# Output projection as seven half-size products, with sums formed by accumulating transfers in device memory

## The chip, the cores and the metric

The kernel runs on one core of a Trainium2 chip. The core has TensorE (PE, matmuls), VectorE (DVE), ScalarE (ACT), GpSimd (POOL) and SyncE (SP), each with an instruction stream of its own that runs in order; SP issues transfers only, POOL and ACT may issue them too. The metric is the device time of one execution in microseconds (us); lower is better.

## The reference, cut to what matters

One layer over 1024 latent tokens and 256 context tokens, model width 1024. A modulated norm and one input projection feed two groups of four heads: retention, and differential attention (the difference of two softmaxes). Their outputs `y`, 1024 tokens x 1024 columns (retention heads first), go through the output projection, are gated and added to `x`; then come a second norm and an MLP.

```python
y_ret_lat = jax.nn.silu(rg_l) * ret_lat.astype(dtype)
...
y_diff_lat = diff_subln(diff_attention(dq_l, k_all, v_all, lam), subln_g, lambda_init)
out_lat = jnp.concatenate([y_ret_lat, y_diff_lat], axis=-1) @ w_out
...
x = x + g1 * y_lat
h2 = rms_norm(x, norm2_g[l]) * (1.0 + sc2) + sh2
x = x + g2 * conv_ffn(h2, w_up[l], conv_w[l], conv_b[l], w_down[l])
```

## The kernel before, in words

All products are float32 made of three passes: an operand is split into a high part (`hi`, cast on ACT) and a remainder (`lo`, subtraction on DVE or POOL), and `passes` (L133 to L135) multiplies hi by hi, lo by hi and hi by lo, one matmul of 128x512 each.

The order in time is: norms and input projection in blocks (0 to 320 us); block 0 with the retention outputs beside it (320 to 400), then another block; differential attention (445 to 643), 32 units, a unit being 128 query tokens of one head; the output projection (L1263 and after, up to 729); up projection, convolution, down projection, final norm. `beside(generator, rate)` puts steps of another job between the matmuls of a running one, `order_only` fixes an order between two instructions without a wait, and a table `TAU` sets at which point of a unit's 5.75 us period each of its operations stands. Each engine then runs its list in order.

*Retention outputs.* For each pair of chunks of one head POOL multiplies the queries (`qq`), raises a variance to the power −1/2 (`ss`) and normalises (`y`); TensorE turns the result, and it is stored in device memory, split into hi and lo, as `yr_d` (one tensor per half of the tokens). During attention four transfers from POOL's queue (`yT<-yrd`, 1 MB each) load it into `yT`.

*Attention.* For each unit DVE forms a mean square (`ssa`, L965), POOL raises it to the power −1/2 (`ssa`, L966), ACT normalises the unit's output with it (`oa`, L969), TensorE turns the result (`pty`, L974), and ACT and DVE write it into `yT[a][half]` (`a`: hi or lo; eight blocks of 128 columns, heads 4 to 7 from attention; 512 tokens). POOL also issues the loads of queries, keys and values (`qhl`, `ks`, `va`), squares a softmax sum per unit (`e`, L962), and loads the first weights of the output projection (`woraw`) and forms their remainders (`wolo`, L1085).

*Output projection.* For each half `n` of the output columns, eight token tiles `t`, eight slices `k` of the width: 2 x 8 tiles of 24 matmuls into one PSUM bank `po`, two banks in turn. The first ones stand between the last units of attention. DVE multiplies a finished tile by the gate (`gated`, L1277) and adds it to the residual `x1[t]` (L1278), which SP loads from `x`; with the second half comes the second norm of those tokens (`norm2`: square on ACT, power on POOL, two scalings on DVE) and a store. `turned0` transposes the first 512 tokens for the up projection beside tiles 4 to 7 of the second half. The MLP adds weights and activations for its own seven-product form with transfers that accumulate: `dma_start(..., accum_op=ALU.add)` on POOL's queue (L1216, `cmb<-w_up`).

## Time and profile before

| what | value |
|---|---|
| median of 3 runs | 1372.66 us (1372.25 to 1372.69) |
| the profiled execution | 1371.83 us, of which its span 1370.1 |
| granted TensorE clock | 0.998 |
| POOL, 470 to 520 us (attention) | 17.17 of 50 us busy |
| ACT, 470 to 520 us | 44.46 of 50 us busy |
| DMA share, 470 to 520 us | 0.82 |
| matmuls | 7026 |

Busy times are those of the core's engines inside the span. A row of a timeline gives start, length, engine, line of the code, operation, destination `<-` sources (numbers of buffers left out), and in brackets how long the engine stood idle before it and what released it. A row of transfers gives size and the median time from issue to landing.

### The profile page before, as it was taken

How to read it: one execution, taken by the hardware profiler on the slowest of the kernel's cores; microseconds unless marked ns; L12 is line 12 of the kernel's file. 1: busy time of each engine (PE TensorE's matmuls, PEld its weight loads, DVE VectorE, ACT ScalarE, POOL GpSimd, SP SyncE). 2: the span in 40 equal slices, each digit the busy share in tenths (PEclk: the TensorE clock that was granted, in tenths of full speed). 3: DMA queues.
4: the chain of work that ended last, by engine and by line, in shares of the span. 5: the costliest groups of instructions: out<-in, count | busy, mean ns of one | idle time of the engine just before them, and what ended most of it. 6: DMA issues, size and time to landing. Idle time of an engine off the chain costs nothing.

```text
span 1370.1 us, 19739 instructions
## 1 busy us (share of the span) xinstructions
PE 1357.6 (99%) x7026; PEld 1144.4 (84%) x7026; DVE 970.5 (71%) x1475; ACT 731.2 (53%) x1397; POOL 304.4 (22%) x395
## 2 busy tenths in 40 slices
PE   9999999999999999999999999999999999999997
PEld 7788888888988899998888888888888888888886
DVE  4755875425776998896457986677766777799857
ACT  4652312424665889986136555455554555454534
POOL 1210004503665424411201222212222210000001
PEclk9999999999999999999999999999999999999999
DMA  9546887654556868623413898888888875963523
GB/s 375 207 170 212 292 305 246 200 175 141 170 169 192 171 174 184 136 47 135 158 50 89 194 227 223 223 224 215 208 223 215 209 189 169 373 220 116 177 92 123
DMA packets 123546, 260.81 MB, mean 190 GB/s; under 512 B 12660, under 2 KB 34164, under 8 KB 122936
## 3 DMA queue, kind: packets, MB, share of 16 engines
q1 hardware_dynamic: 97880, 201.72, 43.5%
q0 software_dynamic: 24992, 56.40, 21.1%
q10 hardware_dynamic: 576, 1.44, 0.3%
q8 instruction: 55, 0.90, 0.3%
q14 instruction: 43, 0.35, 0.1%
HBM read 197.63 MB, written 56.64 MB: 186 GB/s over the span
## 4 chain that ended last, share of the span: by engine, by line
PE 94%; DVE 2%; ACT 2%; DMA 1%; issue 1%; POOL 0%; POOLq 0%; ACTq 0%; DVEq 0%
PE chain L133 6%; PE chain L135 6%; PE chain L134 6%; PE pv L951 5%; PE c L134 5%; PE c L135 5%; PE c L133 5%; PE pA L919 5%; PE pl L135 4%; PE pl L133 4%; PE pl L134 4%; PE pn L135 3%; PE pn L134 3%; PE pn L133 3%; PE third L135 3%; PE third L133 3%
## 5 line engine op out<-in xcount | busy, mean ns | idle before, releaser
L1216 POOL DMA_DIRECT2D cmb<-w_up x80 | 73.6, 1128 | 176.4 <-DMA cmb<-w_up 142.4
L133 PE MATMUL pl<-hT,whi 128*128 128x512 f32 x256 | 105.5, 412 | 0.0
L133 PE MATMUL chain<-T,whi 128*128 128x512 f32 x264 | 103.0, 391 | 0.0
L134 PE MATMUL chain<-T,whi 128*128 128x512 f32 x264 | 102.9, 390 | 0.0
L135 PE MATMUL chain<-T,wlo 128*128 128x512 f32 x264 | 102.4, 389 | 0.0
L922 DVE TENSOR_REDUCE mt<-pA 128x1 f32<-128x1280 f32 x64 | 95.2, 1489 | 7.5 <-PE pA L919 7.1
L135 PE MATMUL pl<-hT,wlo 128*128 128x512 f32 x256 | 100.2, 391 | 0.0
L134 PE MATMUL pl<-hT,whi 128*128 128x512 f32 x256 | 100.0, 391 | 0.0
L135 PE MATMUL c<-whi,ghl 128*128 128x512 f32 x232 | 90.3, 389 | 0.0
L134 PE MATMUL c<-wlo,ghl 128*128 128x512 f32 x232 | 90.3, 389 | 0.0
L133 PE MATMUL c<-whi,ghl 128*128 128x512 f32 x232 | 90.3, 389 | 0.0
L919 PE MATMUL pA<-ks,qhl 128*128 128x512 f32 (+1 forms) x384 | 89.5, 368 | 0.6 <-ACT p L926 0.5
L926 ACT ACTIVATE p<-pA,mt 128x1280 f32<-128x1280 f32 x64 | 85.4, 1335 | 8.5 <-DVE mt L922 8.5
L1139 ACT CAST whi<-cmb 128x512 fp32r<-128x512 f32 x60 | 37.3, 624 | 82.5 <-PE chain L134 66.8
L919 PEld LDWEIGHTS pA<-ks,qhl 128*128 128x128 f32 x384 | 67.9, 189 | 12.7 <-ACT p L926 1.2
L951 PE MATMUL pv<-va,aT 128*128 128x128 f32 x640 | 77.1, 276 | 0.3 <-ACT aT L945 0.2
L951 PEld LDWEIGHTS pv<-va,aT 128*128 128x128 f32 x640 | 74.0, 192 | 1.2 <-ACT aT L945 0.8
L1139 ACT CAST whi<-wra 128x512 fp32r<-128x512 f32 x54 | 33.1, 622 | 72.1 <-PE third L134 42.3
L134 PE MATMUL third<-yT,whi 128*128 128x512 f32 x168 | 65.4, 389 | 0.0
L133 PE MATMUL third<-yT,whi 128*128 128x512 f32 x168 | 65.4, 389 | 0.0
L135 PE MATMUL third<-yT,wlo 128*128 128x512 f32 x168 | 65.4, 389 | 0.0
L133 PE MATMUL pn<-whi,hT 128*128 128x512 f32 x160 | 64.8, 405 | 0.0
(330 smaller groups left out, 3769.1 us busy)
## 6 DMA issues: line engine op xcount, KB each, us to landing
cmb<-w_up POOLq DMA_DIRECT2D x80, 256.0 KB, 6.1
wm<-w_mod SPq DMA_DIRECT2D x32, 512.0 KB, 5.2
cmb<-w_up SPq DMA_DIRECT2D x60, 256.0 KB, 5.3
raw<-w_in SPq DMA_DIRECT2D x27, 512.0 KB, 5.1
wra<-w_up SPq DMA_DIRECT2D x23, 512.0 KB, 5.5
W<-w_down SPq DMA_DIRECT2D x44, 256.0 KB, 5.9
wrb<-w_up SPq DMA_DIRECT2D x40, 256.0 KB, 3.8
ad<-s SPq DMA_DIRECT2D x20, 512.0 KB, 5.2
```

Source lines behind the costliest of these rows:

```text
L133: mm(ps, lh, rh, start=first, stop=False, skip_group_check=more)
L134: mm(ps, lh, rl, start=False, stop=False, skip_group_check=more)
L135: return mm(ps, ll, rh, start=False, stop=last, skip_group_check=more)
L919: mm(self.pa[m][:, c0:c1], self.q[:, m, i, qs], self.k[:, m, c0:c1], start=(i == 0), stop=(i == 1))
L922: nc.vector.tensor_reduce(out=self.mt[:, m : m + 1], in_=self.pa[m][:, :LK], axis=AX.X, op=ALU.min)
L926: nc.scalar.activation(self.p[m], self.pa[m][:, :LK], AF.Exp, scale=-1.0, bias=self.mt[:, m : m + 1], accum_out=self.s[:, m : m + 1])
L951: mm(self.pv, self.aT[:, c, :], self.v[:, c, :], start=(c == 0), stop=(c == NKT - 1))
L1139: cast = nc.scalar.copy(hi, src)
L1216: nc.gpsimd.dma_start(out=o, in_=src, accum_op=ALU.add)
```

## The change

The projection is cut into halves in all three directions: tokens (first and last 512), width (retention and attention heads) and output columns. Seven products of half size, steps A to G of 48 matmuls each, take the place of eight. Each multiplies a sum of blocks of `y` by a sum of blocks of `w_out`:

- *Weight sums.* `ws_d[0..3]` in device memory: four copies of 1 MB issued by SP near 80 us, then eight accumulating transfers of 512 KB on POOL's queue beside the first four tiles of block 0.
- *Token sums.* `sg_d[0..3]`: the retention outputs of the first token half are stored once, unsplit and with turned sign, in `sg_d[0]`; attention outputs of the second token half get their turned sign by the gain `subg[:, 1]`. In attention, `sg_d[2]` is copied from `yr_d` and takes four accumulating transfers of 512 KB, SP copies it to `sg_d[1]` and `sg_d[3]`, and 32 accumulating transfers of 256 KB from `yT` follow on POOL's queue, as heads finish; a head's row of `sg_d[3]` takes four of them, one after another. Two of the four `yT<-yrd` loads go.
- *Steps.* `sum_operand` loads a sum (1 MB) into `raw0` and splits it on ACT and DVE; weights are loaded and split in seven half blocks (28 slices, 16 before). After a step its four banks are gated and added to or subtracted from `x1`: 28 gates, 16 before, four subtractions on POOL. `c1` are four banks (pools `psB`, `psC`), `c2` four (`psA`); steps A, E, F and G go tile by tile, B, C and D run over the slices outside. `turned0` stands beside F and G.

```diff
-    yr_d = [dr.tile([P, 2, H, 512], F32, name=f"yrd{i}") for i in range(2)]
+    yr_d = dr.tile([P, 2, H, 512], F32, name="yrd")
+    sg_d = [dr.tile([P, H, 512], F32, name=f"sgd{i}") for i in range(4)]
+    ws_d = [dr.tile([P, 4, 512], F32, name=f"wsd{i}") for i in range(4)]
+    A11, A12, A21, A22 = [w_out[i][:, c : c + 4, :] for i in range(2) for c in (0, 4)]
...
+                o = self.g % 2 * 2 * P
+                if self.g // 2 == 0:
+                    nc.scalar.mul(r32(yr[:, 0]), pt, -1.0)
+                    nc.sync.dma_start(out=sg_d[0][:, self.h, o : o + 2 * P].rearrange("p (s l) -> p s l", s=2), in_=r32(yr[:, 0]))
+                    return
                 nc.vector.tensor_tensor(out=yr[:, 1], in0=pt, in1=r32(yr[:, 0]), op=ALU.subtract)
-                o = self.g % 2 * 2 * P
-                nc.sync.dma_start(out=yr_d[self.g // 2][:, :, self.h, o : o + 2 * P].rearrange("p a (s l) -> p a s l", s=2), in_=r32(yr))
+                nc.sync.dma_start(out=yr_d[:, :, self.h, o : o + 2 * P].rearrange("p a (s l) -> p a s l", s=2), in_=r32(yr))
...
+        w_copies = [nc.sync.dma_start(out=ws_d[i][:, :, :], in_=a) for i, a in ((0, A21), (1, A11))]
         natural(wget, ctx_lhs, range(NTC), store_to(dv_row))
+        w_copies += [nc.sync.dma_start(out=ws_d[i][:, :, :], in_=a) for i, a in ((2, A11), (3, A12))]
+        for ins, before in zip(w_copies, (-4, -3, -2, -1)):
+            order_only(ins.ins, stops[before].ins)
...
+            for i in range(2):
+                nc.vector.tensor_scalar(out=subg[:, i, :], in0=cl[:, COL_SUB : COL_SUB + H], scalar1=(1 - 2 * i) * (1.0 - LAMBDA_INIT) * SQP, scalar2=None, op0=ALU.mult)
...
-        transposed(wg, None, rtab, 64, 1.0, 0, by_head)
+        w_terms = [(0, A22), (2, A21), (1, ws_d[0]), (3, ws_d[1])]
+
+        def weight_sum(n):
+            if n < 4:
+                i, a = w_terms[n]
+                for k in (0, 2):
+                    added = nc.gpsimd.dma_start(out=ws_d[i][:, k : k + 2, :], in_=a[:, k : k + 2, :], accum_op=ALU.add)
+                    order_only(added.ins, newest[0].ins)
+
+        transposed(wg, None, rtab, 64, 1.0, 0, by_head, each=weight_sum)
...
-    def out_weights(n, sl, eng=nc.sync, low=nc.vector, lag=0):
+    def out_weights(srcs, sl, eng=nc.sync, low=nc.vector, lag=0):
         raws = []
-        for k in range(KD + lag):
-            if k < KD:
+        srcs = [src[:, k, :] for src in srcs for k in range(4)]
...
-    wo_gen = out_weights(0, wo_first, nc.gpsimd, nc.gpsimd, 2)
-
+    wo_gen = out_weights((A11, ws_d[0]), wo_first, nc.gpsimd, nc.gpsimd, 2)
+
+    sums_at = {}
+    for n, src in ((8, yr_d[:, 1]), (10, sg_d[0])):
+        sums_at[n] = [([sg_d[2][:, h : h + 2, :]], src[:, h : h + 2]) for h in (0, 2)]
+    for u in range(3, n_units, 4):
+        h, half = u // NT, u % NT // 4
+        n = {3: 14, 7: 15}.get(u, u + 6)
+        for a in range(2):
+            sums_at.setdefault(n + (2 if u < n_units - 5 else 1) * a, []).append(([sg_d[i][:, h, :] for i in ((1, 0, 3), (3,))[half]], r32(yT[a][half][:, H + h, :])))
+
+    def sum_up(ds, src):
+        for d in ds:
+            nc.gpsimd.dma_start(out=d, in_=src, accum_op=ALU.add)
...
-            if n in (8, 10, 12, 14):
-                a, i = divmod(n // 2 - 4, 2)
+            if n in (8, 10):
                 with tc.issue_after(units[n - 5].pool_ins.ins):
-                    nc.gpsimd.dma_start(out=yT[a][i][:, 0:H, :], in_=yr_d[i][:, a])
+                    nc.gpsimd.dma_start(out=yT[n // 2 - 4][1][:, 0:H, :], in_=yr_d[:, n // 2 - 4])
+            if n == 6:
+                nc.sync.dma_start(out=sg_d[2][:, :, :], in_=yr_d[:, 0])
+            if n == 12:
+                for i in (1, 3):
+                    nc.sync.dma_start(out=sg_d[i][:, :, :], in_=sg_d[2][:, :, :])
+            with tc.issue_after(units[max(0, min(n - 5, n_units - 1))].pool_ins.ins) if n in sums_at else nullcontext():
+                for d, src in sums_at.get(n, ()):
+                    sum_up(d, src)
...
-    psA = ctx_r.enter_context(tc.tile_pool(name="psA", bufs=4, space=PSUM))
+    psA, psC, psB = [ctx_r.enter_context(tc.tile_pool(name=f"ps{nm}", bufs=n, space=PSUM, reuse_waits="tile")) for nm, n in (("A", 4), ("C", 2), ("B", 2))]
+    pst = psA
...
-        for n in range(2):
-            sl = wo_first if n == 0 else []
-            for _ in wo_gen if n == 0 else out_weights(n, sl):
-                pass
-            for t in range(NT):
-                pt = next(out_cycle).tile([P, 512], F32, name="po3", tag="mm")
-                for k in range(KD):
-                    ins = passes(pt, tuple(yT[a][t // 4][:, k, t % 4 * P : (t % 4 + 1) * P] for a in range(2)), sl[k], k == 0, k == KD - 1)
-                    if (n, t) == (0, 0) and k in (0, 7):
-                        order_only(turns[("T1", n_units - 2) if k == 0 else ("Y", n_units - 1)], ins.ins)
-                    tick()
-                dst = x1[t][:, n * 512 : (n + 1) * 512]
-                gated = wo.tile([P, 512], F32, name="gated")
-                nc.vector.tensor_tensor(out=gated, in0=pt, in1=g1[:, n * 512 : (n + 1) * 512], op=ALU.mult)
-                nc.vector.tensor_tensor(out=dst, in0=gated, in1=dst, op=ALU.add)
...
-                if n == 1:
-                    norm2(t)
...
+    rows0, rows1 = x1[:4], x1[4:]
+    left, right = slice(0, 512), slice(512, D)
+    (Y11, Y21), (Y12, Y22) = (B11, B21), (B22, T1)
+    groups = []
+
+    def out_step(cc, a, sl, first, last, by_tile=False):
+        order = [(k, t) for t in range(4) for k in range(4)] if by_tile else [(k, t) for k in range(4) for t in range(4)]
+        for k, t in order:
+            ins = passes(cc[t], tuple(g[:, k, t * P : (t + 1) * P] for g in a), sl[k], first and k == 0, last and k == 3, not first)
+            groups.append(ins)
+            if len(groups) in (1, 8):
+                order_only(turns[("T1", n_units - 2) if len(groups) == 1 else ("Y", n_units - 1)], ins.ins)
+            tick()
+            if by_tile and k == 3:
+                yield t
...
+    def sum_operand(i, tt, half, turn=False):
+        raw = raw0[:, 4 * half : 4 * half + 4, :]
+        nc.sync.dma_start(out=raw, in_=sg_d[i][:, :, :])
+        for k in range(H):
+            if turn:
+                nc.scalar.mul(tt[0][:, k, :], raw[:, k, :], -1.0)
+                nc.vector.scalar_tensor_tensor(out=tt[1][:, k, :], in0=raw[:, k, :], scalar=-1.0, in1=r32(tt[0][:, k, :]), op0=ALU.mult, op1=ALU.subtract)
+            else:
+                split_to(raw[:, k, :], tt, k)
+
+    def gate(dst, src, part, op, eng=nc.vector):
+        gated = wo.tile([P, 512], F32, name="gated", bufs=2)
+        nc.vector.tensor_tensor(out=gated, in0=src, in1=g1[:, part], op=ALU.mult)
+        eng.tensor_tensor(out=dst[:, part], in0=dst[:, part], in1=gated, op=op)
...
+    run(wo_gen)
+    c1 = [(psB if t < 2 else psC).tile([P, 512], F32, name=f"o1_{t}", tag="bank") for t in range(4)]
+    c2 = [psA.tile([P, 512], F32, name=f"o2_{t}", tag="bank") for t in range(4)]
+    run(out_step(c1, Y12, wo_first[:4], True, True, True))
+    sum_operand(2, Y11, 0)
+    w3 = weights(ws_d[3])
+    run(out_step(c2, Y11, wo_first[4:], True, True))
+    for t in range(4):
+        gate(rows1[t], c1[t], left, ALU.add)
+    sum_operand(1, Y12, 1, True)
+    w6 = weights(ws_d[1])
+    for t in range(4):
+        gate(rows0[t], c2[t], right, ALU.subtract)
+    run(out_step(c2, Y21, w3, False, True))
+    w7 = weights(ws_d[2])
+    sum_operand(0, Y11, 0)
+    for t in range(4):
+        gate(rows0[t], c2[t], left, ALU.add)
+    run(out_step(c1, Y12, w6, False, True))
+    w4 = weights(A22)
+    for t in range(4):
+        gate(rows0[t], c1[t], left, ALU.add)
+        done(t, left)
+    sum_operand(3, Y12, 1)
+    pre = [raw_load("wra" if j < 2 else "wrb", w_up[j]) for j in range(NPRE)]
+    early = [[split_op(a[:, c : c + 4, :]) for c in (0, 4)] for a in pre]
+    for t in out_step(c1, Y11, w7, False, True, True):
+        gate(rows0[t], c1[t], right, ALU.subtract)
+        done(t, right)
+        norm2(t)
+    w2 = weights(A12)
+    raws = [up_load(j) for j in range(NSUM)]
+    for a, b in raws:
+        sums_in_place(a, b)
+    beside(turned0(), 0.36, -2.5)
+    for t in out_step(c1, Y12, w4, False, True, True):
+        gate(rows1[t], c1[t], right, ALU.subtract, nc.gpsimd)
+        done(4 + t, right)
+    c1 = [(psB if t < 2 else psC).tile([P, 512], F32, name=f"o3_{t}", tag="bank") for t in range(4)]
+    for t in out_step(c1, Y22, w2, True, True, True):
+        gate(rows1[t], c1[t], left, ALU.subtract)
+        done(4 + t, left)
+        norm2(4 + t)
```

In POOL's list between two powers of attention (units 10 to 12, head 1; 518 to 534 us in the profile). Before:

```order
L1022 DMA va_5275<-dvd_103 128x10x128
L1109 DMA yT11_4470<-yrd1_152 128x2048
L966 TENSOR_TENSOR ssa_5259<-ssa_5259,mhalf_70 128x1
L1078 DMA woraw_5295<-w_out 128x512
L962 TENSOR_TENSOR e_5341<-sa_5061 128x1
L1078 DMA woraw_5369<-w_out 128x512
L962 TENSOR_TENSOR e_5415<-sa_5129 128x1
L966 TENSOR_TENSOR ssa_5338<-ssa_5338,mhalf_70 128x1
L962 TENSOR_TENSOR e_5489<-sa_5200 128x1
L1085 TENSOR_TENSOR wolo_5366<-woraw_5146,wohi_5365 128x512
L1078 DMA woraw_5443<-w_out 128x512
L966 TENSOR_TENSOR ssa_5412<-ssa_5412,mhalf_70 128x1
```

After, from the last of three additions that take the place of the 1 MB load (`yT00`, `yT01`: high part of the first and second token half, `yT10`, `yT11`: remainders):

```order
L1126 DMA sgd3_155<-yT00_4479 128x512
L989 TENSOR_TENSOR ssa_5277<-ssa_5277,mhalf_70 128x1
L1102 DMA woraw_5315<-w_out 128x512
L985 TENSOR_TENSOR e_5361<-sa_5078 128x1
L1102 DMA woraw_5390<-w_out 128x512
L985 TENSOR_TENSOR e_5436<-sa_5146 128x1
L1126 DMA sgd3_155<-yT01_4480 128x512
L989 TENSOR_TENSOR ssa_5358<-ssa_5358,mhalf_70 128x1
L1126 DMA sgd1_153<-yT10_4481 128x512
L1126 DMA sgd0_152<-yT10_4481 128x512
L1126 DMA sgd3_155<-yT10_4481 128x512
L985 TENSOR_TENSOR e_5513<-sa_5218 128x1
```

Additions now stand ahead of and behind the powers; the fourth into this row follows the next power, and after it three more for the next head.

On DVE, the gates of the output projection. Before, at the first three tiles, each tile's product is read and added before the next is gated:

```order
L1278 TENSOR_TENSOR x1_0_6722<-gated_6776,x1_0_6722 128x512
L1277 TENSOR_TENSOR gated_6805<-po3_6780,g1_4474 128x512
L1278 TENSOR_TENSOR x1_1_6723<-gated_6805,x1_1_6723 128x512
L1277 TENSOR_TENSOR gated_6834<-po3_6809,g1_4474 128x512
L1278 TENSOR_TENSOR x1_2_6724<-gated_6834,x1_2_6724 128x512
```

After, between steps B and C, which both write the banks `o2_0` to `o2_3`:

```order
L1340 TENSOR_TENSOR gated_6979<-o2_0_6801,g1_4486 128x512
L1340 TENSOR_TENSOR gated_6982<-o2_1_6802,g1_4486 128x512
L1341 TENSOR_TENSOR x1_0_6774<-x1_0_6774,gated_6979 128x512
L1109 TENSOR_TENSOR wolo_6976<-woraw_6973,wohi_6975 128x512
L1341 TENSOR_TENSOR x1_1_6775<-x1_1_6775,gated_6982 128x512
L1340 TENSOR_TENSOR gated_6985<-o2_2_6803,g1_4486 128x512
L1340 TENSOR_TENSOR gated_6988<-o2_3_6804,g1_4486 128x512
```

A weight remainder and two subtractions stand between the second gate and the third.

At the end of attention, POOL's last powers. Before:

```order
L962 TENSOR_TENSOR e_6645<-sa_6425 128x1
L966 TENSOR_TENSOR ssa_6599<-ssa_6599,mhalf_70 128x1
L962 TENSOR_TENSOR e_6672<-sa_6493 128x1
L966 TENSOR_TENSOR ssa_6642<-ssa_6642,mhalf_70 128x1
L966 TENSOR_TENSOR ssa_6669<-ssa_6669,mhalf_70 128x1
```

After:

```order
L985 TENSOR_TENSOR e_6689<-sa_6465 128x1
L1126 DMA sgd1_153<-yT00_4479 128x512
L1126 DMA sgd0_152<-yT00_4479 128x512
L1126 DMA sgd3_155<-yT00_4479 128x512
L989 TENSOR_TENSOR ssa_6640<-ssa_6640,mhalf_70 128x1
L1126 DMA sgd1_153<-yT10_4481 128x512
L1126 DMA sgd0_152<-yT10_4481 128x512
L1126 DMA sgd3_155<-yT10_4481 128x512
L985 TENSOR_TENSOR e_6719<-sa_6533 128x1
L989 TENSOR_TENSOR ssa_6686<-ssa_6686,mhalf_70 128x1
L989 TENSOR_TENSOR ssa_6716<-ssa_6716,mhalf_70 128x1
```

Six additions of head 3 stand ahead of the last `e`. SP's load of `x1_4`, the first residual of step A, waits for that `e`.

More of the change, by code (lines that the diff above doesn't have):

```diff
@@ L466, in natural_copy, with transposed @@
                 nc.sync.dma_start(out=kvg_d[1 + 2 * hf + i][:, h, 0], in_=st[:, 2 * i : 2 * i + 2, :])
-        def transposed(wget, dst, rtab, blk, scale, col0, order, nat=False, eng=nc.vector):
+        def transposed(wget, dst, rtab, blk, scale, col0, order, nat=False, eng=nc.vector, each=None):
             todo = None
@@ L478, in transposed @@
                 todo = (xa, h, hf) if nat else None
+                if each is not None:
+                    each(2 * h + hf)
             return todo
@@ L908, in __init__ @@
                 self.h, self.qt = divmod(i, NT)
-                self.gain = subg[:, self.h : self.h + 1]
+                self.gain = subg[:, self.qt // 4, self.h : self.h + 1]
                 self.mt = al.tile([P, 2], F32, name="mt", bufs=3)
@@ L1071 @@
     g1 = wo.tile([P, D], F32, name="g1")
-    def out_weights(n, sl, eng=nc.sync, low=nc.vector, lag=0):
+    def out_weights(srcs, sl, eng=nc.sync, low=nc.vector, lag=0):
         raws = []
-        for k in range(KD + lag):
-            if k < KD:
+        srcs = [src[:, k, :] for src in srcs for k in range(4)]
+        for k in range(len(srcs) + lag):
+            if k < len(srcs):
                 raw = wo.tile([P, 512], F32, name="woraw", bufs=4)
-                eng.dma_start(out=raw, in_=w_out[n][:, k, :])
+                eng.dma_start(out=raw, in_=srcs[k])
                 raws.append(raw)
@@ L1082, in out_weights @@
                 whi = wo.tile([P, 512], F32R, name="wohi", bufs=9)
-                wlo = wo.tile([P, 512], F32R, name="wolo", bufs=9)
+                wlo = wo.tile([P, 512], F32R, name="wolo", bufs=8)
                 nc.scalar.copy(whi, raws[k - lag])
@@ L1188, in turned @@
     def turned(hf, d, raw, on_act):
-        pt = pst.tile([P, 512], F32, name="pt3", tag="tr")
+        pt = pst.tile([P, 512], F32, name="pt3", tag="bank")
         for i in range(4):
@@ new lines, in run, with weights @@
+    def run(g):
+        for _ in g:
+            pass
+    def weights(src):
+        sl = []
+        run(out_weights((src,), sl))
+        return sl
+    def sum_operand(i, tt, half, turn=False):
[7 more added lines that the diff above has]
+                split_to(raw[:, k, :], tt, k)
@@ L1291 @@
+    beside(iter(()), 0.0)
     x1lS.close()
@@ L1363 @@
             first[j] = first_sum(chain[j], second[j])
-    pstS.close()
-    psC = ctx_r.enter_context(tc.tile_pool(name="psC", bufs=2, space=PSUM, side="right"))
     ops.append(up_sums(NSUM))
```

22 lines of the change are left out of this document (4 added, 18 removed).

## The prediction

> **What bounds the kernel now.** I read the page first: busy time, then the chain that ended last.
>
> ```profile
> span 1370.1 us, 19739 instructions
> ...
> PE 1357.6 (99%) x7026; PEld 1144.4 (84%) x7026; DVE 970.5 (71%) x1475; ACT 731.2 (53%) x1397; POOL 304.4 (22%) x395
> ...
> PE 94%; DVE 2%; ACT 2%; DMA 1%; issue 1%; POOL 0%; POOLq 0%; ACTq 0%; DVEq 0%
> ```
>
> TensorE is busy for 99% of the span and carries 94% of the chain, so a matmul taken away is time taken away, unless something else then makes TensorE wait. POOL's 22% is an average, and the change loads POOL in two stages only. So next come windows (columns: PE, PEld, DVE, ACT, POOL busy us, granted clock, DMA share, GB/s): one in differential attention, two in the output projection, one in the retention outputs.
>
> ```profile
> 520.00:550.00 30.00, 30.00 (x224) 27.83 (x223) 26.53 (x37) 27.92 (x66) 13.54 (x23) 1.00 0.68 166
> 654.00:680.00 26.00, 26.00 (x117) 21.53 (x116) 11.78 (x16) 3.63 (x6) 8.01 (x6) 1.00 0.39 143
> 680.00:704.00 24.00, 24.00 (x108) 19.88 (x107) 11.22 (x22) 6.80 (x11) 1.64 (x3) 1.00 0.22 77
> 340.00:350.00 10.00, 10.00 (x67) 8.91 (x66) 5.82 (x14) 6.95 (x24) 7.83 (x8) 1.00 0.24 76
> ```
>
> TensorE is full in all four, at full clock. In the projection ACT and DVE have half their time free; in attention ACT has 2.1 us of 30 left, so a late ACT can't catch up there.
>
> **The products.** Sixteen tiles of 24 matmuls (384) become seven steps of 48 (336): 48 fewer. The price of one comes from the VectorE timeline, which ends each tile:
>
> ```profile
> 654.54 0.69 DVE L1277 TENSOR_TENSOR gated<-po,g 128x512 f32<-128x512 f32 x1 [4.02 <-PE po L135]
> 655.26 0.69 DVE L1278 TENSOR_TENSOR x<-gated,x 128x512 f32<-128x512 f32 x1
> ...
> 659.98 0.69 DVE L1277 TENSOR_TENSOR gated<-po,g 128x512 f32<-128x512 f32 x1 [1.91 <-PE po L135]
> ```
>
> Two tiles end 659.98 − 654.54 = 5.44 us apart, 0.227 us a matmul (the 0.39 of a matmul's row is its length in the pipeline). 48 x 0.227 = **−10.9 us**, all of it on the chain.
>
> **Gating between steps.** Gates go from 16 to 28, two VectorE operations of 0.69 each: 24 more, 16.6 us; 12 more weight slices and the token sums are split on ACT and DVE too. They have room: from 654 to 704 DVE is busy 23.0 of 50 us. What counts is the step that writes its banks again at once. Step C adds into the four banks of step B, so each must be read first. B's k-outer order ends its tiles three matmuls (0.68 us) apart, the last at T. DVE gates bank 0 from T − 2.04, bank 1 from T − 1.36, then by its order does the first subtraction (to T + 0.0), a weight remainder that waits for a slot that B frees at T (to T + 0.7), the second subtraction (T + 1.4), and gates 2 (T + 2.1) and 3 (T + 2.8). [...] I take **+1.0**; the ends are 0 (DVE far enough ahead) and 2.8 (all four gates after T). After C, D and A other banks or tile-by-tile order leave the gates at least 2.7 us, so nothing.
>
> **Norms and transposes in steps F and G.** They follow the last gate of E by a chain whose length this shows (gate to second scaled half):
>
> ```profile
> 692.62 0.69 DVE L1277 TENSOR_TENSOR gated<-po,g 128x512 f32<-128x512 f32 x1 [1.06 <-PE po L135]
> ...
> 696.13 0.88 DVE L1184 TENSOR_SCALAR x<-x,sm 128x512 f32<-128x512 f32 x2 [0.66 <-POOL sm L116]
> ```
>
> That is 4.4 us for a row alone; in E rows follow at 2.7 us with weight remainders between. The first transposes stand 30 matmuls (6.8 us) into F. A margin of 2.4 us against one to three DVE operations of 0.69 ahead of the row: 0 to 1.5, I take **+0.5**. POOL's four subtractions in F hold back nobody, since a bank is free once its product is read.
>
> **The token sums in attention.** The new accumulating transfers stand in POOL's queue ahead of the power operation (`ssa`, L966) on which ACT's normalisation of each unit waits. Below: POOL's timeline, then ACT's (the normalisation is L969).
>
> ```profile
> 516.53 0.57 POOL L966 TENSOR_TENSOR ssa<-ssa,mhalf 128x1 f32<-128x1 f32 x1 [3.83 <-DVE ssa L965]
> ...
> 519.28 0.56 POOL L1109 DMA_DIRECT2D yT<-yrd  x1
> 522.28 0.56 POOL L966 TENSOR_TENSOR ssa<-ssa,mhalf 128x1 f32<-128x1 f32 x1 [2.44 <-DVE ssa L965]
> ...
> 528.03 0.57 POOL L966 TENSOR_TENSOR ssa<-ssa,mhalf 128x1 f32<-128x1 f32 x1 [3.69 <-DVE ssa L965]
> ...
> 529.98 1.27 POOL L1085 TENSOR_TENSOR wolo<-woraw,wohi 128x512 fp32r<-128x512 f32 x1 [1.22 <-ACT wohi L1084]
> ...
> 534.25 0.56 POOL L966 TENSOR_TENSOR ssa<-ssa,mhalf 128x1 f32<-128x1 f32 x1 [2.13 <-DVE ssa L965]
> ...
> 539.99 0.56 POOL L966 TENSOR_TENSOR ssa<-ssa,mhalf 128x1 f32<-128x1 f32 x1 [2.39 <-DVE ssa L965]
> ```
>
> ```profile
> 522.78 0.59 ACT L945 COPY aT<-pt 128x512 f32<-128x512 f32 x1 [0.60 <-PE pt L939]
> ...
> 529.79 0.41 ACT L969 ACTIVATE oa<-oa,ssa 128x128 f32<-128x128 f32 x1
> ...
> 541.60 0.41 ACT L969 ACTIVATE oa<-oa,ssa 128x128 f32<-128x128 f32 x1
> ```
>
> Powers are 5.75 us apart. One that ends at 528.60 is used at 529.79, one that ends at 540.55 at 541.60: 1.1 us of slack, and up to 0.6 that ACT idles per unit, say 1.5. Beyond that a late power delays ACT, and TensorE with it. For a transfer that adds into memory the rows of the MLP are nearest: L1216 issues the same size (256 KB), first its issue time in ns, then its time to land.
>
> ```profile
> L1216 POOL DMA_DIRECT2D cmb<-w_up x80: 857/886/1904, 753.1 to 1116.2; - x80
> ...
> DMA to landing us min/median/max: 3.2/5.9/10.2
> ```
>
> ```profile
> wrb<-w_up POOLq DMA_DIRECT2D x2, 256.0 KB, 4.1
> ...
> cmb<-w_up POOLq DMA_DIRECT2D x5, 256.0 KB, 5.1
> ...
> woraw<-w_out POOLq DMA_DIRECT2D x8, 256.0 KB, 3.8
> ...
> yT<-yrd POOLq DMA_DIRECT2D x1, 1024.0 KB, 10.0
> ```
>
> Issue, 0.87: POOL has it free (13.5 busy of 30). The wait is what matters. In `sgd3` one head takes four additions, and each waits in POOL's queue for the one before to land. For head 0 the first stands where the 1 MB load of 519.28 stood, behind the same key, query and value loads, and that landed 10.0 later, at 529.3. The second is issued then, so the power due at 528.03 comes at 530.2: 2.2 late, 0.7 lost. The third waits for a landing again, with 2.0 us of work behind it (1.27 + 0.6 + 0.2) ahead of the power due at 534.25; the fourth likewise, with 4.7 us behind it (a load, a remainder, and three additions of head 1) ahead of that due at 539.99. With 3.7 us from end of issue to landing (between the 3.2 of the pair at 4.1 and the 4.2 of the five at 5.1, less 0.87) these lose 0.4 and 1.4. Together **+2.5**. Ends: 0, with 2.3 us to land (the minimum of L1216) and a first addition that isn't late; 12, with 7 us. Each microsecond of landing costs up to 3, one for each wait. Heads 1 to 3 have an interval more between their additions and lose nothing below 6 us.
>
> The page "DMA: Bandwidth & Descriptors" of the Trainium skill (section "Anatomy of one DMA — SWDGE (gpsimd) path") gives such a transfer 2.0 us plus its bytes at 436 GB/s, an estimate of 2.6 us for 256 KB. By it the additions would cost nothing after the first 0.7 and the sum would end near 1365; the rows here, 4.1 and 5.1, are longer, so it stands among the rivals.
>
> **End of attention.** The load of `x1_4` waits for POOL's last `e` (L962), which now stands behind three more additions.
>
> ```profile
> 633.66 0.19 POOL L962 TENSOR_TENSOR e<-sa 128x1 f32<-128x1 f32 x1
> ...
> 633.88 1.28 SPq L1175 DMA_DIRECT2D x<-x  x3
> ...
> 641.94 0.16 DVE L965 SCALAR_TENSOR_TENSOR ssa<-e,ssa 128x1 f32<-128x1 f32 x1 [2.75 <-ACT jka L960]
> ...
> x<-x SPq DMA_DIRECT2D x8, 512.0 KB, 5.5
> ```
>
> 3 x 0.87 puts the load at 636.5, its landing at 642.0, and DVE's first residual addition, which now stands ahead of the last unit's `ssa`, ends at 642.7, where `ssa` was due at 641.94: **+0.8**, nothing hides it, since TensorE's last transpose of attention hangs on it. Ends 0 and 2.5: ACT also gets four casts of a 1 MB load ahead of its last copies, and that load (10.0 at its slowest above) has some 7 us.
>
> **The weight sums.** Eight additions of 512 KB go between the first retention outputs, where POOL is busy 7.83 of 10 us: two issues of 0.87 in a 5.7 us stretch exceed the 1.2 free, and one pair waits for a landing. The query products stand a unit ahead, which is the cover. 0 to 3 (one landing), I take **+0.6**. The four 1 MB copies near 80 us and the smaller stores: nothing, the weight slices there are fetched ahead; if that cover goes, at most the 5.5 us of one late load (the row of `x<-x` above).
>
> **Sum**, from the profiled execution's 1371.83: −10.9 + 1.0 + 0.5 + 2.5 + 0.8 + 0.6 = −5.5, 1366.3. The median of the runs is 0.83 above it, so **1367**.
>
> **Rivals.** (1) Additions land fast: up to 3 us after issue, and the first is not late. The plain 3.8 of `woraw` in this very stage speaks for it, the accumulating rows against it. 1371.83 − 10.9 + 2.9 = 1363.8, 1364.7 by the median. (2) Additions land in 4.7 to 6.5 us: the chain of `sgd3` gives 5.3 to 10.7 back, no change, some 1370 to 1375. The 5.9 median (5.0 after issue) speaks for it, though it comes from a busier stage. (3) The other side: the same place, head 0, with over 6.5 us per landing. The gain is then gone, above 1375.5, 1377 with 7 us (12 lost). The group's 10.2 maximum shows that it can be.
>
> **Chances.** 0.2% (2.7 us) is about what a measurement can tell from no change. Forecast (1365 to 1369.9) 0.47; rival 1 0.21; rival 2 0.19; rival 3 0.13. Faster 0.68, same 0.19, slower 0.13. From 1363 to 1374.5 leaves out the best of rival 1 (0.05) and the worst of 2 and 3 (0.15).
>
> **What would show it.** In the profile after: 336 projection matmuls at 0.227; TensorE idle about 1 us between B and C; powers near 530, 537 and 544 late by one to three us with POOL waiting for `sgd3` ahead of them. Wrong, if TensorE has no idle time at all in attention, or if its idle time lies in the retention outputs, where I have put only 0.6.

## The result, and the profile after

The changed kernel takes **1395.66 us** (median of 6 runs, 1386.74 to 1396.85) where the kernel before takes 1372.64 (6 runs): ratio 1.0154, 95% interval 1.0127 to 1.0181. It is slower by 23 us; 1367 was forecast. The profiled execution after took 1396.85 us with a span of 1395.1, 25.0 more than before; its mean granted clock is 0.988 (0.998 before). The six runs spread over 10 us, those of the kernel before over 3, and the profile is of the slowest.

The page after, the same lines as before:

```profile
span 1395.1 us, 19873 instructions
...
PE 1358.2 (97%) x6978; PEld 1142.4 (82%) x6978; DVE 997.7 (72%) x1516; ACT 748.0 (54%) x1425; POOL 356.1 (26%) x441
...
PE 83%; DMA 7%; DVE 3%; issue 3%; ACT 2%; POOL 2%; SPq 0%; POOLq 0%; ACTq 0%; DVEq 0%
```

48 matmuls are gone (7026 to 6978), and TensorE is busy no shorter. Its share of the chain falls from 94% to 83%, and DMA has 7% where it had 1%. So TensorE now stops. The rows of its timeline that follow an idle time of over 2 us (start, length, engine, line, what it computes, and in brackets the idle time and what ended it):

```profile
273.13 1.23 PE L350 MATMUL pu<-kvs,ks 128*128 128x128 f32 x4 [3.83 <-ACT ks L334]
...
548.32 0.69 PE L962 MATMUL pt<-ident,p 128*128 128x128 f32 x2 [6.57 <-ACT aT L968]
...
670.31 0.48 PE L997 MATMUL pty<-ident,oa 128*128 128x128 f32 x1 [5.80 <-ACT oa L992]
...
731.66 0.33 PE L1233 MATMUL pt<-ident,x 128*128 128x128 f32 x1 [2.26 <-DVE x L1226]
```

Before, no stop after 60 us was longer than 0.7. All of TensorE's idle times after its first matmul add to 26.3 us, against 3.6 before: 22.7 more. That isn't the whole price. Windows of after, three of them right behind a stop (the granted clock stands after the busy times), and one inside the seven products:

```profile
273.00:277.00 4.00, 3.87 (x11) 3.29 (x12) 2.05 (x7) 2.75 (x5) 0.00 (x0) 0.50 0.84 250
277.00:281.00 4.00, 4.00 (x17) 3.31 (x17) 0.70 (x2) 1.04 (x2) 0.00 (x0) 0.76 0.73 249
548.00:552.00 4.00, 3.68 (x14) 3.29 (x15) 3.30 (x4) 2.41 (x7) 2.70 (x4) 0.50 1.03 126
670.00:675.00 5.00, 4.69 (x12) 3.73 (x13) 1.00 (x3) 0.62 (x2) 0.88 (x1) 0.51 0.79 290
680.00:704.00 24.00, 24.00 (x107) 19.71 (x106) 21.24 (x35) 12.19 (x21) 0.86 (x1) 1.00 0.95 311
```

```profile
273.00:277.00 4.00, 4.00 (x24) 3.41 (x23) 0.70 (x2) 1.56 (x3) 0.00 (x0) 1.00 0.98 331
548.00:552.00 4.00, 4.00 (x34) 3.83 (x33) 3.32 (x6) 3.69 (x9) 1.59 (x3) 1.00 0.22 66
```

The second fence is the kernel before: 24 matmuls begin from 273 to 277, after the stop 11 do. Behind each of these stops TensorE counts as busy but runs at half clock for 3.4 to 5.8 us (0.76 is a mean: 0.50 up to 278.9, 1.00 from there). The clock missing from 1 in such stretches, times their length, is 2.9 us behind the stop at 273, 1.7 behind shorter ones near 465 (1.30 and 0.47), 1.8 behind 548, 2.3 behind 670 and 1.7 behind 732: 10.4 together. The ledger of the profiled execution is then −10.9 (products) + 22.7 (idle) + 10.4 (slow clock) + 1.6 (the span goes on 4.4 us past the last instruction, 2.8 before, not pursued) = 23.8 of the 25.0 measured.

**The stop at 548** is the place of the third rival. POOL's timeline, from the first addition to `sgd3` on:

```profile
528.57 1.83 POOL L1126 DMA_DIRECT2D sgd<-yT  x2
531.45 0.84 POOL L1126 DMA_DIRECT2D sgd<-yT  x1 [1.05 <-DMA sgd<-sgd]
532.02 0.87 POOL L989 TENSOR_TENSOR ssa<-ssa,mhalf 128x1 f32<-128x1 f32 x1
...
544.55 0.91 POOL L1126 DMA_DIRECT2D sgd<-yT  x1 [10.17 <-DMA sgd<-yT]
545.17 0.88 POOL L989 TENSOR_TENSOR ssa<-ssa,mhalf 128x1 f32<-128x1 f32 x1
...
548.99 0.85 POOL L1126 DMA_DIRECT2D sgd<-yT  x1 [1.19 <-DMA sgd<-yT]
...
554.92 0.89 POOL L1126 DMA_DIRECT2D sgd<-yT  x1 [2.13 <-DMA sgd<-yT]
```

The first addition, issued at 531.45, landed 13 us later; POOL's next addition waited for it, and with it the power due some 5.75 us after 532.02, which came at 545.17. ACT's normalisation waits for that power, TensorE for ACT. Transfers issued in this stretch (size, median time to landing). After, from 526 to 532, and the copies that SP issued at 518:

```profile
sgd<-yT POOLq DMA_DIRECT2D x3, 256.0 KB, 13.2
ks<-dk POOLq DMA_DIRECT2D x1, 640.0 KB, 12.2
va<-dvd POOLq DMA_DIRECT2D x1, 640.0 KB, 12.9
qhl<-dq POOLq DMA_DIRECT2D x1, 512.0 KB, 9.4
...
sgd<-sgd SPq DMA_DIRECT2D x2, 12.1
```

Before, the same three loads, issued from 517 to 519.2:

```profile
ks<-dk POOLq DMA_DIRECT2D x1, 640.0 KB, 7.6
va<-dvd POOLq DMA_DIRECT2D x1, 640.0 KB, 8.6
qhl<-dq POOLq DMA_DIRECT2D x1, 512.0 KB, 5.2
```

Everything on POOL's queue lands late there, the loads as well as the additions. The additions don't make the loads late: experiment 6 has none of the 40, and the same loads, issued from 518 to 520, take

```profile
ks<-dk POOLq DMA_DIRECT2D x1, 640.0 KB, 11.2
va<-dvd POOLq DMA_DIRECT2D x1, 640.0 KB, 11.9
qhl<-dq POOLq DMA_DIRECT2D x1, 512.0 KB, 8.7
```

What it has in common with the changed kernel is SP's two copies `sgd<-sgd` of 1 MB, issued 8 to 9 us ahead of these loads (12.0 us to landing there). They are the likely cause; no run leaves them out.

Over the whole program the additions land in 7.1 us:

```profile
sgd<-yT POOLq DMA_DIRECT2D x32, 256.0 KB, 7.1
...
wsd<-w_out POOLq DMA_DIRECT2D x4, 512.0 KB, 9.5
wsd<-wsd POOLq DMA_DIRECT2D x4, 512.0 KB, 8.5
```

**The stop at 670** comes from the same wait in head 3: its second three additions wait for the first (POOL), the loads of `x1` for POOL's `e` behind them (SP), DVE's addition of `x1_4` for those loads, and the last unit's power for DVE:

```profile
657.50 0.88 POOL L1126 DMA_DIRECT2D sgd<-yT  x1 [3.30 <-DMA sgd<-yT]
```

```profile
660.92 1.81 SPq L1217 DMA_DIRECT2D x<-x  x3
```

```profile
668.43 0.69 DVE L1341 TENSOR_TENSOR x<-x,gated 128x512 f32<-128x512 f32 x1 [8.74 <-DMA x<-x]
669.04 0.15 DVE L988 SCALAR_TENSOR_TENSOR ssa<-e,ssa 128x1 f32<-128x1 f32 x1
```

ACT had what the last unit's mean square (`ssa`) needs ready at 662.4, so it came 6.6 late. Before, the load was issued 8.1 us ahead of that operation (633.88 and 641.94), now 1.5 ahead of the time at which it was due.

**The stop at 273** is no stage that the prediction looked at. POOL idles there, so it issues the first two weight additions as soon as their order allows, at 260, and the load of `w_in` that ACT needs next comes late (POOL, then ACT):

```profile
260.27 1.79 POOL L911 DMA_DIRECT2D wsd<-w_out  x2
```

```profile
271.14 1.04 ACT L197 CAST whi<-raw 128x1024 fp32r<-128x1024 f32 x1 [7.16 <-DMA raw<-w_in]
```

**The stop at 732**: POOL's powers of the second norm (`sm`, L116) stand in its queue behind six in-place sums of MLP weights. The first three wait for a load until 707.17; the other three, below, keep the first power until 722.76, 2.8 us after what it needs is there. The powers of the next three rows wait for DVE, which has weight remainders between the rows, so the sums explain only part of this stop:

```profile
717.73 2.01 POOL L1292 TENSOR_TENSOR wrb<-wrb 128x512 f32<-128x512 f32 x1 [0.39 <-DMA wrb<-w_up]
719.81 1.29 POOL L1293 TENSOR_TENSOR wra<-wrb,wra 128x512 f32<-128x512 f32 x1
721.18 1.61 POOL L1294 TENSOR_TENSOR wra<-wra 128x512 f32<-128x512 f32 x1
722.76 0.56 POOL L116 TENSOR_TENSOR sm<-sm,mhalf 128x1 f32<-128x1 f32 x1
```

### The profile page after: what moved, and what is told of

Its sections match the earlier page's. It is cut to its first block, busy times and chain, and to the rows that moved or that the text cites. A ratio compares the mean times of both kernels' runs of the same rounds, so it can differ in the third digit from the quotient of the medians.

```text
span 1395.1 us, 19873 instructions
## 1 busy us (share of the span) xinstructions
PE 1358.2 (97%) x6978; PEld 1142.4 (82%) x6978; DVE 997.7 (72%) x1516; ACT 748.0 (54%) x1425; POOL 356.1 (26%) x441
## 3 DMA queue, kind: packets, MB, share of 16 engines
q10 hardware_dynamic: 576, 1.44, 0.3%
## 4 chain that ended last, share of the span: by engine, by line
PE 83%; DMA 7%; DVE 3%; issue 3%; ACT 2%; POOL 2%; SPq 0%; POOLq 0%; ACTq 0%; DVEq 0%
PE chain L133 6%; PE chain L134 6%; PE chain L135 6%; PE c L135 5%; PE c L133 5%; PE c L134 5%; PE pl L133 4%; PE pl L135 4%; PE pl L134 4%; PE pA L942 3%; PE pn L135 3%; PE pn L133 3%; PE pn L134 3%; PE pv L974 3%; PE third L134 3%; PE third L133 3%
```

## The experiments

The theory: an addition costs time only where something that TensorE needs soon stands behind its issue or its landing, so moving the additions removes the stops though the same bytes move. The rival: the additional traffic costs some 20 us wherever it stands. Line numbers shift by a few between the kernels; ratios are to runs of the kernel before on the same chip. Experiments 1 to 3 differ from the changed kernel by less than its own spread of 10 us, so they are read by their traces.

**1. Weight additions one tile later** (`e1_weights_later`).

```diff
-            if n < 4:
-                i, a = w_terms[n]
+            if 1 <= n < 5:
+                i, a = w_terms[n - 1]
```

> One edit to the changed kernel: the eight weight additions are issued one tile of block 0 later, so the first two no longer start at 260 us, beside the last input-projection weight loads. Theory (waits in queues that run in order, each followed by a spell of half TensorE clock): the 3.8 us stop at 269 us goes, with some 3 us of half clock behind it, so 6 to 7 us less than the changed kernel, near 1389. Rival (the added bytes cost wherever they are put): the loads they meet later are late instead, 1394 to 1397.

Measured: 1391.49 us, ratio 1.0132 (1.0116 to 1.0147). The stop at 273 is gone, and loads from `w_in` land in 5.5 us at the median (6.3 in the changed kernel). Three stops of 1.07, 1.01 and 0.87 came instead at 207, 368 and 379, with the clock at 1.00 behind them. The start of attention came 2.1 us earlier. So the early pair did make that stop, but most of its idle time came back in small pieces.

**2. Token additions spread** (`e2_sums_spread`): a head's four additions to `sgd3` three units apart, so that each has landed long before the next.

```diff
-        n = {3: 14, 7: 15}.get(u, u + 6)
...
+    sums_from = (14, 18, 25, 37)
...
+                n = sums_from[h] + (3 if h < 3 else 1) * (2 * half + a) - (1 if h == 3 and half else 0)
```

> One edit to the changed kernel: the same 32 token additions, but those into one row stand three units apart (17 us), and head 3's come behind the last power of attention. Theory of waits: the stops at 541, 560 to 563 and 664 us (14.6 us) go, with 6 to 9 us of half clock, so 20 to 23 us less, 1373 to 1376. Rival (traffic of the accumulating transfers delays the key, query and value loads and x1): nothing gained by moving them, above 1388. If the first addition alone is at fault, half of it.

Measured: 1393.26 us, ratio 1.0143 (1.0128 to 1.0158). The same 32 additions, as slow to land (7.5 at the median), stop TensorE nowhere in attention behind its first units: from its first to its last unit 202.6 us pass, 220.8 in the changed kernel, 201.2 before. For attention this decides for the theory. The total hardly moved (13.3 us of the 18.2 are lost again between the last unit and the end of step G, 2.2 ahead of attention, where the stop at 273 is 4.62 here), since the last additions, put behind the last power, now hold back `raw0`, the operand of the second step. ACT's timeline, then TensorE's:

```profile
676.60 2.19 ACT L1334 ACTIVATE yT<-raw 128x512 fp32r<-128x512 f32 x4 [16.55 <-DMA raw<-sgd]
678.70 2.52 ACT L1108 CAST wohi<-woraw 128x512 fp32r<-128x512 f32 x4
```

```profile
679.35 0.79 PE L133 MATMUL o<-wohi,yT 128*128 128x512 f32 x1 [8.43 <-ACT wohi L1108]
```

The first step's weight cast stands behind the waiting cast in ACT's order: 8.43 us of stop, and 4.53 later at a gate behind DVE. One late landing can be moved about without any gain.

**3. Norm powers ahead of the in-place weight sums** (`e3_sums_after_norms`).

```diff
+        added_up = nc.gpsimd.tensor_tensor(out=b1, in0=b1, in1=b2, op=ALU.add)
+        order_only(added_up.ins, powers[3].ins)
```

> One edit to the changed kernel: in POOL's queue the four powers of the second norm of the first 512 tokens stand ahead of the in-place weight sums of the MLP, which wait for a load. Theory: the stop of 2.3 us at 729 us and part of the 0.4 at 758 go, with 1 to 2 us of clock, so 3 to 5 us less, 1391 to 1393. Rival (VectorE, busy all of 700 to 720, is what is late): within 1 us of the changed kernel, 1395 to 1397.

Measured: 1397.66 us (1393.63 to 1401.66), ratio 1.0185 (1.0162 to 1.0208), not better. The stop of 2.26 became one of 1.28, and stops of 2.52 and 1.28 came 22 us later, in the later transposes. That the sums delay the powers is shown; they make at most part of the stop, and this order doesn't mend it.

**4. The same transfers without addition** (`e4_plain`): the 32 token transfers overwrite, in the same queue and order.

```diff
-            nc.gpsimd.dma_start(out=d, in_=src, accum_op=ALU.add)
+            if len(ds[0].shape) == 2:
+                nc.gpsimd.dma_start(out=d, in_=src)
```

> The 32 token transfers write instead of adding: same sources, destinations, queue, order and waits, so the token sums are left incomplete. If adding to device memory is what makes a landing 7 to 13 us long, plain writes land in 3 to 4 us and the stops at 541 and 664 us shrink to 0 to 3 us, time 1374 to 1382. If the queue ahead and the traffic make it long, landings stay at 6 us or more and the time above 1388.

Measured: 1384.15 us, ratio 1.0074 (1.0054 to 1.0093).

```profile
sgd<-yT POOLq DMA_DIRECT2D x32, 256.0 KB, 4.4
```

Adding is what makes 4.4 into 7.1 us. Attention takes 208.5 us, 12.3 less than with additions; the stop at its end is gone. But the stop in head 0 stays, at 5.07 us, and its first three transfers still take 12.7 us to land (median), so that one is made by what stands ahead of them, not by the addition. Four issued from 541.77 on, when that is over, land in 2.5 us (median).

**5. The places changed together** (`e5_rearranged`): weight additions at retention tile 1 and in attention units 26 and 29; token additions spread as in 2, head 3's earlier; the second half's operand read after step C; the MLP's first loads and in-place sums ahead of step D. By a slip of the bound in `n < n_units` it leaves out the last pair of weight additions (`wsd3`).

```diff
+        weight_at = (1, 26, 29, 32)
...
+            if n > 20 and n < n_units:
+                with tc.issue_after(units[n - 5].pool_ins.ins):
+                    weight_sum(n)
...
-    sum_operand(1, Y12, 1, True)
...
     run(out_step(c2, Y21, w3, False, True))
+    sum_operand(1, Y12, 1, True)
```

> The changed kernel with the same products and sums, put elsewhere: only the first pair of weight additions stays in the retention outputs (one tile later), the other three pairs go beside units of heads 2 and 3; token additions into one row stand three units apart; of head 3 only the first three stand ahead of the last powers; the load of the turned sum is issued after step C's products; the MLP's first weight loads and in-place sums stand ahead of step D. Theory of waits: no stop above 1 us is left, and the 10.9 us of the products show, 1362 to 1367. Rival (each addition costs where it stands, by bytes or by another wait): above 1372.7.

Measured: 1369.19 us, ratio 0.9979 (0.9970 to 0.9987), clock 0.998. 38 of the 40 additions are still there; the stops left after 60 us are 1.72 at the first gates, 1.40 in the transposes and none over 0.7 elsewhere. Nearly all of the loss is a matter of places.

**6. None of the 40 additions** (`e6_no_adds`) leaves out the 8 of weights and the 32 from `yT`, so the sums are incomplete; the copies, the four early additions into `sgd_d[2]`, the loads and the seven products stay.

```diff
-            if n < 4:
+            if n < 0:
```

> The changed kernel without the 8 weight additions and the 32 additions from yT (the sums are left incomplete; copies, the four early token additions, products, gates and splits stay). Theory: what the additions cost goes, the products' 10.9 us show, less the 2.3 us stop before the transposes and its clock: 1363 to 1367. Rival (the seven-step projection itself waits for its weights, splits or banks): 1370 or more.

Measured: 1369.59 us, ratio 0.9980 (0.9971 to 0.9989). That bounds this arrangement: without the 40 additions only 2.7 of the 10.9 us are left (0.2% of 1372); experiment 9, with two edits more, has 4.8 (0.35%). The two stops of this kernel, in TensorE's timeline:

```profile
683.99 0.47 PE L133 MATMUL o<-wohi,yT 128*128 128x512 f32 x1 [1.21 <-DVE gated L1341]
...
705.86 0.33 PE L1234 MATMUL pt<-ident,x 128*128 128x128 f32 x1 [3.56 <-DVE x L1227]
```

After the second, the clock is 0.50 from 707.3 to 710.7, 1.7 us lost. The seven-product form itself takes back most of what it saves, by its gates and by the norm ahead of the transposes.

**7. One stop, alone** (`e7_one_stop`): the kernel *before*, with nine useless multiplications of 128x512 on POOL ahead of unit 11's power.

```diff
+                    for k in range(9):
+                        held = nc.gpsimd.tensor_tensor(out=spin, in0=spin, in1=spin, op=ALU.mult)
```

> The kernel before, with nine POOL multiplications of 128x512 that nobody needs (1.27 us each) ahead of one power of attention (unit 11), so that this power comes some 7.8 us late, as the late additions make it. Theory: TensorE stops for about 6 us and then runs some 4 to 5 us at half clock, 2 to 3 us more: 8 to 9 us in all, 1380 to 1382. Rival (a stop costs only its own length): 1378 to 1379.

Measured: 1380.02 us, ratio 1.0061 (1.0045 to 1.0076), 8.0 us more. The power comes at 535.58 (528.03 before). TensorE's timeline, then windows behind the second stop (0.93 is a mean; the clock is back at 1.00 from 541.4):

```profile
531.74 2.50 PE L951 MATMUL pv<-va,aT 128*128 128x128 f32 x20 [1.11 <-DVE yT L990]
...
538.41 0.69 PE L939 MATMUL pt<-ident,p 128*128 128x128 f32 x2 [4.18 <-ACT aT L945]
```

```profile
538.00:541.00 3.00, 2.59 (x8) 2.20 (x9) 1.85 (x3) 2.50 (x7) 0.66 (x2) 0.50 0.25 87
541.00:544.00 3.00, 3.00 (x23) 2.83 (x22) 2.70 (x3) 2.15 (x5) 1.70 (x4) 0.93 0.32 56
```

5.3 us of stops and 0.50 x 3 + 0.07 x 3 = 1.7 of slow clock make 7.0; the span is 7.1 longer. No transfer was touched, so a late power on POOL is enough for the stop, and the stop for the slow clock. The page "TensorE: Matmul & The Clock Gate" of the Trainium skill (section "Part 1: The HAM clock gate") says that a TensorE idle for a window of some 3.4 us falls to half clock until it has been busy as long. The stops of 3.5 us and more here agree. Shorter ones went both ways: 1.30 and 0.47 us near 465 in the changed kernel, and 2.10 and 2.07 alone in experiments 8 and 10, were followed by some 3 us at 0.50, while 3.00 us in experiment 9 and 1.72 in 5 left the clock at 1.00.

**8 to 11. Towards a complete version in attention.** `e8_rearranged2` is 5 with the last weight pair at unit 32, step C tile by tile and the transposes later; `e9_no_adds_later_turns` is 6 with the same two edits; `e10_weights_early` is 8 with the pairs at units 22, 26 and 30, `wsd3` ahead of `wsd2`; `e11_low_on_pool` is 10 with eight weight remainders on POOL.

```diff
-    run(out_step(c2, Y21, w3, False, True))
+    run(out_step(c2, Y21, w3, False, True, True))
...
-    beside(turned0(), 0.36, -2.5)
+    beside(turned0(), 0.5, -7.0)
```

> e5_rearranged with its last pair of weight additions (wsd3, which e5 left out) beside the last unit, and two edits at the stops that e5 and e6 still showed: step C goes tile by tile, so that its banks are wanted 2.7 us apart, and the transposes for the up projection begin 18 matmuls (4 us) later in step F. Theory: the stops on the gates (1.2 to 2.4 us) and before the transposes (1.4 to 3.6 us) go with their half clock, 1363 to 1366. Rival (VectorE and ScalarE are then too full in steps F and G, the stop moves behind them): 1368 to 1371.

> e6_no_adds (sums left incomplete) with the same two edits: step C tile by tile, transposes 18 matmuls later. It bounds what the seven products can give here. Theory: of e6's 1369.6 the stops of 1.2 and 3.6 us and 2 us of half clock go, 1362 to 1365. Rival (the stop moves to the transposes of the last 512 tokens): 1367 to 1370.

> e8_rearranged2 with the weight additions in another order and earlier (the sum that step C reads lands near 610 us, not 632), so that no cast of it waits in ScalarE's queue in front of attention's last copies. Theory (e8's stop of 3.5 us at 630 us, its half clock and the late landings after it are that wait): 4 to 7 us less than e8, 1371 to 1374. Rival (the additions' bytes at the end of attention): as e8, 1377 to 1380.

> e10 with the remainders of eight weight slices (steps E and F) on POOL in place of VectorE, 5.5 us less on VectorE between 660 and 720 us. Theory (the stops of 1 to 2 us before steps with new gates are VectorE being behind): two of three stops go, 2 to 4 us less than e10. Rival (POOL, at 1.27 us each and with additions in its queue, gives the remainders later than VectorE did): 1 to 5 us more than e10.

Measured: 8, 1379.09 us (ratio 1.0050, 1.0036 to 1.0063); 9, 1367.80 (0.9965, 0.9952 to 0.9979); 10, 1378.06 (1.0039, 1.0026 to 1.0052); 11, 1382.13 (1.0071, 1.0058 to 1.0085). In 8 a cast of the first weights waits 3.72 us for `woraw<-wsd`, and TensorE stops for 3.50 near 632; in 10 a stop of 3.95 came near 604 in its place. In 11 a stop of 6.39 came at 702, behind ACT's split of an operand, which waited 6.12 for its load: more work on POOL was no help. In 9 the transposes' stop fell from 3.56 to 1.76, but a stop of 3.00 came in the first units of attention.

**12. A complete version** (`e12_complete`): 5 with all additions, `wsd0`, `wsd1` and `wsd3` at retention tiles 1, 3 and 5, `wsd2` at unit 30.

```diff
-        w_terms = [(0, A22), (2, A21), (1, ws_d[0]), (3, ws_d[1])]
+        w_terms = [(0, A22), (1, ws_d[0]), (3, ws_d[1]), (2, A21)]
+        weight_at = (1, 3, 5, 30)
```

> The changed kernel with every addition kept and only their places changed: weight additions for wsd0, wsd1 and wsd3 at retention tiles 1, 3 and 5, wsd2's at attention unit 30; the token additions spread over the heads; the second half's operand of step D read after step C; the MLP's first loads and in-place sums ahead of step D. Theory (an addition costs time only through the TensorE stop that its landing makes, and each stop about 1.5 times its length): no wait for raw (about 270 us) nor in attention's heads, so the stops left are those of e5_rearranged, 1.7 at the gate and 1.4 in the transposes, with about 1 us near 206 as in e1_weights_later: 1369 to 1372 us. Rival (32 token and 8 weight transfers cost some 6 us wherever they stand, as e10_weights_early's 1378.1 suggests): 1376 to 1380 us, with a new stop of 3 us or more where the landings next fall.

Measured: 1373.50 us (11 runs), the kernel before 1373.02 (15 runs): ratio 1.0005 (0.9995 to 1.0015), clock 0.998. No stop is over 1.7 us:

```profile
461.12 0.44 PE L965 MATMUL pt<-ident,p 128*128 128x128 f32 x2 [1.56 <-DVE xa L453]
...
666.83 0.50 PE L133 MATMUL o<-wohi,yT 128*128 128x512 f32 x1 [1.62 <-DVE gated L1347]
...
709.38 0.33 PE L1240 MATMUL pt<-ident,x 128*128 128x128 f32 x1 [1.44 <-DVE x L1233]
```

It lies between the two expectations, nearer to the theory's 1372 than to the rival's 1376. With every addition kept, 22 us of the loss are gone; in the profiled execution the projection is 6.1 us shorter than before (82.5 for 88.6), attention 2.5 longer, what is ahead of it 2.7 and what follows 2.1 longer. Against the products' −10.9 the span is 12 us too long (1371.3 for 1370.1): TensorE's idle times, in stops of up to 1.6 us, make 7.3 of it (10.9 for 3.6 before), and the stretch behind its last matmul 1.7; the rest isn't assigned. Why the 1.56 near 461 (0.66 before, and 0.68 in 5) grew wasn't settled. No kernel tried computes everything and beats the kernel before.

Of the twelve expectations, only that of 7 came out in its theory's range. 1, 4, 5, 6 and 12 came out between theory and rival; 2, 9, 10 and 11 in the rival's range (2 by a wait that neither named); 3 and 8 outside both.

## Why the prediction was wrong, by its own steps

| step | forecast | idle measured | slow clock behind it |
|---|---|---|---|
| products | −10.9 | −10.9 by the count | |
| gating of step C | +1.0 (0 to 2.8) | 0 | |
| norms and transposes | +0.5 (0 to 1.5) | 2.7 | 1.7 |
| token sums, head 0 | +2.5 (0 to 12) | 8.8 | 1.8 |
| end of attention | +0.8 (0 to 2.5) | 5.8 | 2.3 |
| weight sums | +0.6 (0 to 3) | 4.4 | 2.9 |
| near 465 (no step) | | 0.6 | 1.7 |

The idle column adds the stops of over 0.3 us that belong to a step, less what stood there before.

- *The products held.* 107 matmuls in the 24 us of the window from 680 are 0.224 us each, where 0.227 was taken.
- *The gates cost nothing in the changed kernel*, which the range allows, but the account of them fails elsewhere. Where the large stops ahead were gone, TensorE stopped at the start of step C for bank 0, not bank 2 (1.62 us in 12, 1.72 in 5, with 0.67 and 0.66 for bank 3 behind), and at the start of step E (1.17 to 2.10 in 6, 8, 9 and 10), where the prediction had "at least 2.7 us, so nothing". No run shows a signal from DVE to TensorE that would take 0.2 of the +1.0: at the stop of 732 DVE's scaling ends at 731.61, and the matmul starts at 731.66.
- *The token sums failed in the landing.* This is the largest miss. The step "with 3.7 us from end of issue to landing" took plain transfers and an MLP stage for a price that the additions here don't have: 4.4 plain, 7.1 adding. Its other half, that the first addition lands at 529.3, took issue and landing of the load that it replaced and put nothing on SP's two copies. With the 9.3 us by which the loads ahead of it were issued late (526.36 for 517.06) that is 538.6. It waited for a copy to land, was issued at 531.45 behind two other additions and loads that were late themselves, and landed at 544.3, so the second addition, and the power behind it, came some 6 us later than even that. The third rival named this place and the right sign, but from 1375.5, not 1396.
- *The end of attention failed in the chain.* "3 x 0.87 puts the load at 636.5" counts the issues of three additions (2.6 us) and not that the next three wait for their landing (3.30, 0.42). So the load came 6.6 us later against the last unit, not 2.6, and it landed in 7.5, not 5.5: from the margin of 2.6 that becomes 6.0, and 0.7 for the addition itself.
- *The weight sums failed in the place.* "Eight additions go between the first retention outputs" put them where the code stands; POOL, idle there, issued the first pair 60 us earlier. The order that I read shows what follows what, and not when.
- *The norms failed in the queue.* The step counted DVE's operations ahead of a row, and for POOL only the subtractions. The in-place sums stood ahead of the powers too, and they wait for a load. With the sums out of the way 1.28 to 1.44 remain there (3, 5, 12), and 3.56 came in 6 with the sums in their place, so DVE's part was sized low too.
- *No step priced the clock.* Each stop was taken as its own length; behind five of them another 1.7 to 2.9 us are lost, 10.4 in all. Even with every stop sized right, the sum would have been 10 us short.
- *The sign that was named* ("or if its idle time lies in the retention outputs") came in part: the first stop lies ahead of them.

The prediction's estimate by the page "DMA: Bandwidth & Descriptors" of the Trainium skill, 2.6 us for such a transfer, is off by more than its own rows were: no addition from `yT` landed in under 3.9 us, and their median is 7.1. Plain transfers came down to it in experiment 4, in the four from 541.77 on (2.5). The measurement decides.

## What to carry to other kernels

A transfer put into the queue of an engine that also computes is priced by what stands behind it, in both directions: the small operation that another engine awaits, and the next transfer that waits for the first to land; give a chain of additions to one place several landings of distance, and order it behind the operations that others wait for. On an engine that idles, an instruction runs when its order allows and not where the code stands, so look for the first moment at which it can issue and what it meets there. A stop of TensorE of about 3.5 us or more costs its length and some 2 us of half clock, so a saving of 11 us in products is gone with two of them.

## What the runs showed of the hardware beyond what was expected

- Adding into device memory made 256 KB transfers land in 7.1 us instead of 4.4 at the median (the changed kernel and experiment 4), and its issue on POOL took 0.9 us instead of 0.56.
- Behind every stop of 3.5 to 8.4 us the granted clock was 0.50 for some 3 to 6 us and then 1.00 (5.6 us at 0.50 from 273.2 in the changed kernel, 3 us from 538.4 in experiment 7). Single stops of 2.07 and 2.10 us did the same (10 and 8), and one of 3.00 us did not (9).
- Loads of keys, queries and values in POOL's queue took 12.2, 9.4 and 12.9 us where they had taken 7.6, 5.2 and 8.6, and 11.2, 8.7 and 11.9 without the 40 additions (6). In both cases two 1 MB copies from SP's queue were under way, which took 12 us themselves.
- Two additions of 512 KB on POOL's queue, issued at 260.3, stood beside a load of `w_in` from SP's queue that landed after 10.3 us (4.4 before).
